# Attention and mLSTM stretch of a hybrid decoder layer: merge by quarters on two engines, masks and loads placed elsewhere

## Chip, cores and metric

One Trainium2 chip, one of its cores. The metric is the device time of one execution in microseconds (us). Engines: PE is TensorE (PEld its weight loads), DVE is VectorE, ACT is ScalarE, POOL is GpSimd, SP is SyncE, whose queue issues almost all DMAs of this kernel.

## What is computed

One layer for 2048 tokens of width 1024, all in float32. A combined projection of the normalised input feeds two groups: 8 attention heads of 128 with three dilated windows that are merged by their softmax denominators, and 4 mLSTM heads of 256 in chunks.

```python
u = jnp.einsum("bsd,de->bse", rmsnorm(x, norm_g), w_in)
q_a, k_a, v_a, z_a, x_m, o_m, z_m = jnp.split(u, cuts, axis=-1)
...
for window, dilation in ((128, 1), (512, 4), (2048, 16)):
    o, l = dilated_window_attention(heads(q_a), heads(k_a), heads(v_a), window, dilation, slopes)
wts = jax.nn.softmax(jnp.stack(lses), axis=0)
att = jnp.sum(wts[..., None] * jnp.stack(outs), axis=0).reshape(B, S, D_ATT)
att = att * jax.nn.silu(z_a)
...
hm = mlstm_chunkwise(mh(q_m), mh(k_m), mh(v_m), log_i, log_f)
hm = jax.nn.sigmoid(mh(o_m)) * hm
hm = (hm - mu) * lax.rsqrt(var + NORM_EPS) * hn_g
mls = hm.reshape(B, S, D_MLSTM) * jax.nn.silu(z_m)
return rmsnorm(x + jnp.einsum("bse,ed->bsd", jnp.concatenate([att, mls], -1), w_out), final_g)
```

## The kernel before

Three stages follow each other. The input projection (lines 348 to 520) leaves q, k, v, the gates and the mLSTM operands in DRAM. Then comes the stretch that the change is about: `attention` and `mlstm` are two Python generators, and the main loop takes one step of the first, then as many steps of the second as `total` (the number of steps that `mlstm` has) spreads over 204 of them. Last comes the output projection (lines 1078 to 1120).

**Attention.** A head has 32 steps: 16 blocks of queries, each once with its near keys and once with the strided ones, which hold the two longer windows in one row. A step makes the scores (`qk`, L741 to L747), turns the row two steps earlier over (`flip`, L755) and multiplies with v (`pv`, L773). The near part ends up in `oL`, the strided part in `oR`, both 128 x 2048. Three steps after a head is done `head_stats` turns the row sums over, sends them to DRAM and back in another order (`st_d`, `sL`, `sR`), and makes two weights for each token (`w`, L809), which go to DRAM (`wm_d`, L810). `head_merge` loads them back, copied to all 128 partitions (`wb`, L820), in two halves of 1024 tokens. For each half DVE does four operations of 128 x 1024: `oL` times its weight (L824), `oR` times its weight (L826), their sum (L829), and the gate `zs` times the sum (L834), which reads and writes every fourth element; then `att_d` is stored (L835). `wb` is one buffer, so the second half is loaded when the first has been used. The merge of a head runs while the next head's steps go on.

**mLSTM.** There are 16 chunks of 128 tokens, and two units in each, of two heads. `load` (L912 to L923) fetches five operands from DRAM: `v`, `q`, `xc`, `nb` (two rows of gate numbers copied to all partitions) and `ot`. `unit` makes a causal mask on GpSimd (`E`, L930), takes its exponential on ScalarE (L934), scales q on GpSimd (`qs`, L937), multiplies the mask with the scores (L944), and does the products with the state `C` (L961 to L981). `norm` finishes a chunk: small DVE operations on 128 x 4 (L987 to L999, with `rsqrt`, L84 to L93), four `hm` scalings of 128 x 256 (L1003), then per unit the load of the gate `z` (L1009), four transposes on PE (L1013), a product on DVE (L1014) and a store (L1015).

The order on each engine is set by a scheduler at build time, from the order in which the code issues the instructions and from its own durations. On the chip each engine and the SP queue go through their lists in that order: an instruction that waits holds up all that stand behind it on its engine. All tiles are guarded by semaphores that the build puts in.

The lines that the prediction speaks of most:

```python
820  nc.sync.dma_start(wb[:, i], wm_d[h][i:i + 1, :]...[:, :, cs].to_broadcast([128, 4, 256]))
826  nc.vector.tensor_tensor(v, v, wb[:, 1], ALU.mult)
834  nc.vector.tensor_tensor(zq, zq, o.rearrange("p r q -> p q r"), ALU.mult)
930  nc.gpsimd.affine_select(E, nb[:, :, 0, :], pattern=[[0, 2], [1, 128]], ...)
1003 nc.vector.tensor_scalar(hm, hm, sm[:, 0, h:h + 1], sm[:, 3, h:h + 1], op0=ALU.add, op1=ALU.mult)
```

Of the kernel before, what the change touches and what calls it, by code (L numbers as in the profile page):

```python
# [16 lines left out]
T = 2048  # L17
# [10 lines left out]
def kernel(  # L28
# [782 lines left out]

    def head_merge(at, d):
        h = d["h"]
        oL, oR, zs = d["oL"], d["oR"], d["zs"]
        for hf in range(2):
            cs = slice(hf * 256, (hf + 1) * 256)
            t0 = hf * 1024
            wb = at.tile([128, 2, 4, 256], F32, name="wb")
            for i in range(2):
                nc.sync.dma_start(wb[:, i], wm_d[h][i:i + 1, :].rearrange("p (r q) -> p r q", r=4)[:, :, cs]  # L820
                                  .to_broadcast([128, 4, 256]))
# [5 lines left out]
            yield  # L827
# [4 lines left out]
            z = zs[:, t0:t0 + 1024]  # L832
            zq = z.rearrange("p (q r) -> p q r", r=4)
            nc.vector.tensor_tensor(zq, zq, o.rearrange("p r q -> p q r"), ALU.mult)  # L834
            nc.sync.dma_start(att_d[h][:, t0:t0 + 1024], z)  # L835
            yield

    def attention(at):
# [9 lines left out]
        for i in range(len(units) + 3):  # L848
            if i < len(units):
                h, u = units[i]  # L850
                if i == 0:
                    by_r.append(at.tile([128, 2, 2, 512], F32R, name="oL", bufs=2))
                    D_[0] = head_tiles(at, first_load)
                    D_[0]["kh"] = at.tile([128, T], F32R, name="wb")
                    qk_split(D_[0], 0)
                S_[i] = qk(at, D_[h], u)
# [31 lines left out]
            if merges and (i % 32 == 10 or i % 32 > 14) and next(merges[0], "end") == "end":  # L888
                merges.pop(0)
# [11 lines left out]
    def mlstm(mp):  # L901
        C = mp.tile([128, KT, 257], F32, name="C")
        L = {}
        Z = {}
# [3 lines left out]
        def load(c, p):  # L908
            cs = slice(c * 128, (c + 1) * 128)
            es = slice(4 * p, 4 * p + 4)  # L910
            v = mp.tile([128, 2, 257], F32, name="v", bufs=2)
            nc.sync.dma_start(v[:, :, 0:256], vm_d[cs, p * 512:(p + 1) * 512].rearrange("t (i d) -> t i d", i=2))  # L912
            nc.gpsimd.memset(v[:, :, 256:257], 1.0)
# [4 lines left out]
            nb = mp.tile([128, 2, 2, 128], F32, name="nb", bufs=2)  # L918
            for i in range(2):
                nc.sync.dma_start(nb[:, i].rearrange("p a t -> p (a t)"),  # L920
                                  nb_d[(2 * p + i) * 16 + c].rearrange("a t -> (a t)")[None, :].to_broadcast([128, 256]))
            ot = mp.tile([128, 512], F32, name="ot", bufs=2)
            nc.sync.dma_start(ot, o_d[cs, p * 512:(p + 1) * 512])  # L923
            L[c, p] = (v, q, xc, nb, ot)

        def unit(c, p):
            v, q, xc, nb, ot = L.pop((c, p))
            sm = SM[c]
            E = mp.tile([128, 2, 128], F32, name="E")
            nc.gpsimd.affine_select(E, nb[:, :, 0, :], pattern=[[0, 2], [1, 128]], compare_op=ALU.is_ge,  # L930
                                    fill=-BIG, base=0, channel_multiplier=-1)
            for i in range(2):
                j = (2 * p + i) * 16 + c
                nc.scalar.activation(E[:, i], E[:, i], AF.Exp, bias=gcol[:, 0, j:j + 1])  # L934
            if c:
                qs = mp.tile([128, 4, 128], F32, name="qs")
                nc.gpsimd.tensor_tensor(qs.rearrange("p (i e) t -> p i e t", e=2), q.rearrange("p (i e) t -> p i e t", e=2),  # L937
                                        nb[:, :, 1, None, :].to_broadcast([128, 2, 2, 128]), ALU.mult)
# [6 lines left out]
            yield  # L945
            if c < NB - 1:
# [24 lines left out]
            for i in range(2):  # L971
                j = (2 * p + i) * 16 + c
                for e in range(2):
                    if c < NB - 1:
# [5 lines left out]
                        else:  # L980
                            nc.vector.tensor_copy(ce, u[:, 0:257])  # L981
                    yield

        def norm(c):
            sm = SM[c]
            hms = [HM.pop((c, p)) for p in range(2)]
            nc.vector.reciprocal(sm[:, 1, :], sm[:, 1, :])  # L987
# [17 lines left out]
            cs = slice(c * 128, (c + 1) * 128)  # L1005
            for p in range(2):
                es = slice(4 * p, 4 * p + 4)
                z = mp.tile([128, 4, 128], F32, name="z", bufs=2)
                nc.sync.dma_start(z, zm_d[es, :, cs].rearrange("e p t -> p e t"))  # L1009
                yield  # L1010
# [3 lines left out]
                nc.vector.tensor_tensor(z, z, ps, ALU.mult)  # L1014
                nc.sync.dma_start(mls_d[es, :, cs].rearrange("e p t -> p e t"), z)  # L1015
                yield

        load(0, 0)
        tail = None
        for c in range(NB):  # L1020
            SM[c] = mp.tile([128, 4, MH], F32, name="sm", bufs=2)
            for p in range(2):
                nxt = (c, 1) if p == 0 else (c + 1, 0)
                if nxt[0] < NB:
                    load(*nxt)
                for n, _ in enumerate(unit(c, p)):
# [11 lines left out]

# [43 lines left out]
    def out_fin(pss, b):  # L1082
        xr = at.tile([128, 2, D], F32, name=("zs", "wb")[b % 2])[:, 0]
# [22 lines left out]
    def out_last(pss, b):  # L1106
        xr = at.tile([128, 2, D], F32, name=("zs", "wb")[b % 2])[:, 0]
# [153 lines left out]
```

## Time and profile before

| | |
|---|---|
| time, median of 3 runs | 2215.12 us (2212.78 to 2215.84) |
| the profiled execution | 2221.72 us |
| span of its instructions | 2219.9 us |
| busy: PE, DVE, ACT, POOL | 2101.2 (95%), 1466.3 (66%), 923.1 (42%), 173.2 (8%) us |
| mean granted TensorE clock | 0.983 of full speed |
| DMA | 332.70 MB, mean 150 GB/s |

Busy time is an average over the stages. Attention and mLSTM run from about 1241 to 1800 us of the span; the last head and the first products of the output projection reach to about 1905 us. A row of the chain of waits names what ended each wait; idle time of PE is what the sections below look for.

### The profile page before, as it was taken

The page shows a single profiled execution, that of the slowest core. Times are in us where ns is not written, and L with a number is a line of the kernel's source. Part 1 is how long each engine was busy: PE and PEld are TensorE (multiplying, and loading weights), DVE is VectorE, ACT ScalarE, POOL GpSimd, SP SyncE. Part 2 cuts the span into 40 slices and gives each one's busy share as a digit, 9 for nine tenths or more (in the row PEclk, how much of TensorE's full clock was granted, in tenths as well). Part 3 has the DMA queues.
Part 4 walks back from the last instruction along what each step waited for, and adds up shares of the span by engine and source line. Part 5 has one row for each costly group of instructions (what it writes and reads, how often), then busy time and mean ns, then how long its engine had stood idle before and what let it go on. Part 6 is the DMA issues. An engine that isn't in the chain of part 4 may idle for free.

```text
span 2219.9 us, 32081 instructions
## 1 busy us (share of the span) xinstructions
PE 2101.2 (95%) x11762; PEld 1780.5 (80%) x11762; DVE 1466.3 (66%) x2969; ACT 923.1 (42%) x1873; POOL 173.2 (8%) x187
## 2 busy tenths in 40 slices
PE   5999999999999999999999898998889979899998
PEld 4677878998888888787789887888888877788886
DVE  8888767656696458586666567877877866442322
ACT  6433333333383223334344565665565664211111
POOL 2200000000000000000000212222222210000000
PEclk9999999999999999999999999999999999999999
DMA  4255343433253333343324767878779846543221
GB/s 153 95 177 188 114 158 119 154 115 109 81 204 133 114 114 107 123 143 121 122 77 159 192 169 224 239 217 238 196 220 238 224 152 196 158 133 95 95 91 38
DMA packets 300717, 332.70 MB, mean 150 GB/s; under 512 B 19536, under 2 KB 241168, under 8 KB 298512
## 3 DMA queue, kind: packets, MB, share of 16 engines
q1 hardware_dynamic: 299696, 330.06, 47.9%
q8 instruction: 93, 1.52, 0.3%
q10 hardware_dynamic: 864, 0.59, 0.1%
q14 instruction: 64, 0.52, 0.1%
HBM read 221.87 MB, written 108.72 MB: 149 GB/s over the span
## 4 chain that ended last, share of the span: by engine, by line
PE 76%; DVE 9%; DMA 8%; ACT 3%; issue 2%; SPq 1%; POOL 1%; ACTq 0%; DVEq 0%; POOLq 0%
PE pb L348 34%; PE pa L348 13%; PE pm L773 3%; DMA wb<-wm_d 2%; PE pt L755 2%; DMA nb<-nb_d 1%; PE pu L1078 1%; PE pu L1079 1%; PE pu L1080 1%; PE aux L493 1%; PE aux L503 1%; PE pt L1080 1%; PE pt L1078 1%; PE pt L1079 1%; PE pq L1080 1%
## 5 line engine op out<-in xcount | busy, mean ns | idle before, releaser
L97 ACT ACTIVATE whi<-ws 128x1024 fp32r<-128x1024 f32 x140 | 148.2, 1059 | 377.7 <-PE pb L348 211.8
L98 DVE TENSOR_TENSOR wlo<-ws,whi 128x1024 fp32r<-128x1024 f32 x140 | 171.9, 1228 | 81.7 <-ACT whi L97 81.6
L138 DVE TENSOR_TENSOR ws<-w,w 128x1024 f32<-128x1024 f32 x140 | 172.2, 1230 | 24.9 <-DMA w<-in_w_in 23.2
L747 ACT ACTIVATE s<-s,st 128x256 f32<-128x256 f32 (+3 forms) x256 | 134.9, 527 | 82.6 <-DVE st L745 75.3
L410 DVE TENSOR_TENSOR o<-pb,o 128x1024 f32<-128x1024 f32 x84 | 102.8, 1224 | 95.0 <-PE pb L348 93.9
L745 DVE CUSTOM_DVE_ANT_0 s<-pq,bl 128x256 f32<-128x256 f32 (+3 forms) x256 | 114.4, 448 | 39.1 <-PE pq L743 18.3
L755 PE MATMUL pt<-sc,s 128*128 128x128 f32 x568 | 109.7, 284 | 22.2 <-DVE E L944 7.3
L97 ACT ACTIVATE whi<-w 128x1024 fp32r<-128x1024 f32 x56 | 59.2, 1057 | 123.0 <-PE pb L348 116.6
L760 ACT ACTIVATE p<-pt 128x256 f32<-128x256 f32 (+1 forms) x192 | 80.9, 422 | 70.2 <-PE pt L755 68.0
L410 DVE TENSOR_TENSOR o<-pa,o 128x1024 f32<-128x1024 f32 x56 | 68.4, 1221 | 61.4 <-PE pa L348 61.4
L755 PEld LDWEIGHTS pt<-sc,s 128*128 128x128 f32 x568 | 72.8, 145 | 34.1 <-ACT p L760 9.1
L773 PE MATMUL pm<-p,vc 128*128 128x128 f32 x640 | 97.2, 283 | 2.1 <-ACT p L760 1.3
L605 POOL COPY bl<-bl 128x256 f32<-128x256 f32 x8 | 6.1, 757 | 1136.9 <-DMA q<-q_d 1111.6
L976 PE MATMUL pu<-v,kw 128*128 128x257 f32 x240 | 74.2, 404 | 19.9 <-DVE C L979 13.9
L403 ACT ACTIVATE o<-pb 128x1024 f32<-128x1024 f32 x84 | 85.0, 1017 | 17.2 <-DVE o L410 9.5
L773 PEld LDWEIGHTS pm<-p,vc 128*128 128x128 f32 x640 | 85.3, 198 | 5.2 <-ACT p L760 3.2
L98 DVE TENSOR_TENSOR wlo<-w,whi 128x1024 fp32r<-128x1024 f32 x56 | 68.3, 1220 | 27.5 <-ACT whi L97 27.5
L773 PE MATMUL pm<-p,vn 128*128 128x128 f32 x496 | 80.0, 283 | 2.8 <-ACT p L760 2.8
L482 DVE SCALAR_TENSOR_TENSOR y<-o,cw,y 128x512 f32<-128x512 f32 x96 | 72.1, 751 | 2.5
L773 PEld LDWEIGHTS pm<-p,vn 128*128 128x128 f32 x496 | 68.3, 197 | 4.9 <-ACT p L760 4.7
L348 PE MATMUL pa<-h4h,whi 128*128 128x512 f32 x160 | 66.8, 417 | 1.0 <-ACT h4h L97 1.0
L348 PE MATMUL pa<-h7l,whi 128*128 128x512 f32 x160 | 64.1, 401 | 2.4 <-DVE h7l L98 2.4
(730 smaller groups left out, 6501.4 us busy)
## 6 DMA issues: line engine op xcount, KB each, us to landing
w<-in_w_in SPq DMA_DIRECT2D x112, 512.0 KB
wb<-wm_d SPq DMA_DIRECT2D x32, 512.0 KB
q_d<-o SPq DMA_DIRECT2D x8, 1024.0 KB
k_d<-o SPq DMA_DIRECT2D x16, 512.0 KB
vm_d<-vm SPq DMA_DIRECT2D x32, 256.0 KB
xc_d<-xc SPq DMA_DIRECT2D x32, 256.0 KB
qm_d<-qm SPq DMA_DIRECT2D x32, 256.0 KB
v_d<-o SPq DMA_DIRECT2D x8, 1024.0 KB
```

Source lines behind the costliest of these rows:

```text
L97: nc.scalar.activation(hi, raw, AF.Copy)
L98: nc.vector.tensor_tensor(lo, raw, f(hi), ALU.subtract)
L138: eng.tensor_tensor(s, a, b, ALU.add if sign > 0 else ALU.subtract)
L348: nc.tensor.matmul(out, lhsT, rhs, start=start, stop=stop, skip_group_check=True)
L403: nc.scalar.activation(dst, order(ps), AF.Copy)
L410: nc.vector.tensor_tensor(dst, ps, src, op)
L745: nc.vector.tensor_tensor_reduce(s[:, :n], ps[:, :n], bias, 1.0, 3e38, ALU.add, ALU.min, accum_out=st[:, col:col + 1])
L747: nc.scalar.activation(s[:, :n], s[:, :n], AF.Exp, bias=st[:, col:col + 1], scale=-1.0, accum_out=st[:, 16 + col:17 + col])
L755: nc.tensor.transpose(pp[:, i * 128:(i + 1) * 128], s[:, i * 128:(i + 1) * 128], ident)
L760: nc.scalar.activation(p[:, :n], pp[:, :n], AF.Copy)
L773: nc.tensor.matmul(od, v, p[:, j * 128:(j + 1) * 128], start=j == 0, stop=j == m - 1)
L976: nc.tensor.matmul(u[:, 0:257], kw[:, 2 * i + e, :], v[:, i], start=True, stop=True)
```

## The change

The merge of a head goes by four quarters of 512 tokens (`weights_load`, L812 to L816, and `head_merge`). `wb` has two smaller buffers; the first two quarters are loaded before any is used, the others when a buffer is free. `oL` times its weight and the sum stay on DVE (now L831 and L839, 128 x 512); `oR` times its weight and the gate times the sum go to GpSimd (L832 and L842). The store of a quarter is issued in the next one (L837, L844). The merge goes on at every step from the tenth of a head.

In `mlstm`, `load` is issued after the second step of the unit before, in the order `nb`, `q`, `xc`, `v`, `ot` (L925 to L934); `v` has two fixed buffers, whose column of ones is set once and not each time. The mask and `qs` move from the unit's start into `prepare` (L940, L944), called late in the unit before, with two buffers each. `norm` loads `z` at its start (L1010), scales `hm` on GpSimd (L1028), and issues its stores (L1038) two steps later. `total` follows: a chunk now has 26 steps and not 25. The keys' copy `kh` of the first head, and two tiles of the last stage, take other buffers.

```diff
+    def weights_load(at, d, n):
+        wb = d["wb", n] = at.tile([128, 2, 4, 128], F32, name="wb", bufs=2)
+        for i in range(2):
+            nc.sync.dma_start(wb[:, i], wm_d[d["h"]][i:i + 1, :].rearrange("p (r q) -> p r q", r=4)
+                              [:, :, n * 128:(n + 1) * 128].to_broadcast([128, 4, 128]))
...
-        for hf in range(2):
...
-            wb = at.tile([128, 2, 4, 256], F32, name="wb")
...
-            nc.vector.tensor_tensor(o, o, wb[:, 0], ALU.mult)
-            yield
-            nc.vector.tensor_tensor(v, v, wb[:, 1], ALU.mult)
...
-            nc.vector.tensor_tensor(o, o, v, ALU.add)
...
-            nc.vector.tensor_tensor(zq, zq, o.rearrange("p r q -> p q r"), ALU.mult)
-            nc.sync.dma_start(att_d[h][:, t0:t0 + 1024], z)
+        weights_load(at, d, 0)
+        yield
+        weights_load(at, d, 1)
+        yield
+        yield
+        for n in range(4):
...
+            nc.vector.tensor_tensor(o, o, wb[:, 0], ALU.mult)
+            nc.gpsimd.tensor_tensor(v, v, wb[:, 1], ALU.mult)
+            yield
+            if n < 2:
+                weights_load(at, d, n + 2)
+            if n:
+                nc.sync.dma_start(att_d[h][:, (n - 1) * 512:n * 512], zs[:, (n - 1) * 512:n * 512])
+            yield
+            nc.vector.tensor_tensor(o, o, v, ALU.add)
+            zq = zs[:, ts].rearrange("p (q r) -> p r q", r=4)
+            yield
+            nc.gpsimd.tensor_tensor(zq, zq, o, ALU.mult)
+            yield
+        nc.sync.dma_start(att_d[h][:, 1536:2048], zs[:, 1536:2048])
...
-            if merges and (i % 32 == 10 or i % 32 > 14) and next(merges[0], "end") == "end":
+            if merges and i % 32 >= 10 and next(merges[0], "end") == "end":
...
+        V = [mp.tile([128, 2, 257], F32, name=f"v{n}") for n in range(2)]
+        for v in V:
+            nc.gpsimd.memset(v[:, :, 256:257], 1.0)
...
+        def prepare(c, p):
+            q, nb = L[c, p][1], L[c, p][3]
+            E = mp.tile([128, 2, 128], F32, name="E", bufs=2)
+            nc.gpsimd.affine_select(E, nb[:, :, 0, :], ...)
+            qs = mp.tile([128, 4, 128], F32, name="qs", bufs=2)
+            if c:
+                nc.gpsimd.tensor_tensor(qs..., q..., nb[:, :, 1, None, :]..., ALU.mult)
...
             nc.vector.tensor_tensor(E, E, ps[:, 0:2, :], ALU.mult)
             yield
+            if nxt:
+                load(*nxt)
...
+                    if nxt and i == 1 and e == 0:
+                        prepare(*nxt)
                     yield
...
+            for p in range(2):
+                z = mp.tile([128, 4, 128], F32, name="z", bufs=2)
+                nc.sync.dma_start(z, zm_d[4 * p:4 * p + 4, :, cs].rearrange("e p t -> p e t"))
...
-                nc.vector.tensor_scalar(hm, hm, sm[:, 0, h:h + 1], sm[:, 3, h:h + 1], op0=ALU.add, op1=ALU.mult)
+                nc.gpsimd.tensor_scalar(hm, hm, sm[:, 0, h:h + 1], sm[:, 3, h:h + 1], op0=ALU.add, op1=ALU.mult)
...
-    total, done, start, end, lag = 16 * 25, 0, 18, 222, 5
+    total, done, start, end, lag = 16 * 26, 0, 18, 222, 5
```

What the build makes of it is seen in the engines' lists. DVE, the merge of the fourth head (its first half before, its first quarter now), before:

```order
L824 TENSOR_TENSOR oL<-oL,wb 128x4x256
L745 ISA s,st<-pq,bl 128x256
L745 ISA st 128x1
L826 TENSOR_TENSOR oR<-oR,wb 128x4x256
L965 SCALAR_TENSOR_TENSOR hm,sm<-ot,pu 128x256
L968 SCALAR_TENSOR_TENSOR sm<-pu,gcol 128x1
L997 TENSOR_SCALAR sm<-sm 128x4
```

and now:

```order
L831 TENSOR_TENSOR oL<-oL,wb 128x4x128
L745 ISA s,st<-pq,bl 128x256
L745 ISA st 128x1
L1021 SCALAR_TENSOR_TENSOR sm<-sm 128x4
L839 TENSOR_TENSOR oL<-oL,oR 128x4x128
L959 TENSOR_TENSOR E<-E,pt 128x256
```

L826 and L834 are gone from this list; the sum L839 stands one step (one L745) behind the product, and it takes `oR` from GpSimd.

GpSimd, the first merge and the unit before it, now (before, only the mask, `qs`, the casts L616 and a memset stood here):

```order
L1028 TENSOR_SCALAR hm<-hm,sm 128x256 x4
L940 AFFINE_SELECT E<-nb 128x256
L944 TENSOR_TENSOR qs<-q,nb 128x512
L832 TENSOR_TENSOR oR<-oR,wb 128x4x128 x2
L842 TENSOR_TENSOR zs<-zs,oL 128x4x128
L616 COPY qr<-qh 128x512
L832 TENSOR_TENSOR oR<-oR,wb 128x4x128
L842 TENSOR_TENSOR zs<-zs,oL 128x4x128
L616 COPY qr<-q 128x512
L832 TENSOR_TENSOR oR<-oR,wb 128x4x128
L842 TENSOR_TENSOR zs<-zs,oL 128x4x128
L940 AFFINE_SELECT E<-nb 128x256
```

The casts of q for the strided rows and the next mask now stand between and behind operations that wait for `wb` and for DVE.

SP, from the store of the fourth head's weights on, before:

```order
L810 DMA wm_d_85<-w 64x2x32
L1015 DMA mls_d<-z 128x4x128
L1009 DMA z<-zm_d 128x4x128
L915 DMA q<-qm_d 128x4x128
L820 DMA wb<-wm_d_85 128x4x256 x2
L1015 DMA mls_d<-z 128x4x128
L912 DMA v<-vm_d 128x2x256
L917 DMA xc<-xc_d 128x4x128
L920 DMA nb<-nb_d 128x256 x2
```

and now:

```order
L810 DMA wm_d_85<-w 64x2x32
L1038 DMA mls_d<-z 128x4x128
L925 DMA nb<-nb_d 128x256 x2
L815 DMA wb<-wm_d_85 128x4x128 x4
L1038 DMA mls_d<-z 128x4x128
L815 DMA wb<-wm_d_85 128x4x128 x2
L1010 DMA z<-zm_d 128x4x128 x2
L928 DMA q<-qm_d 128x4x128
L930 DMA xc<-xc_d 128x4x128
L932 DMA v_10237<-vm_d 128x2x256
L934 DMA ot<-o_d 128x512
```

`nb` goes first and `v` late; the third quarter of `wb`, which waits for a free buffer, stands ahead of the loads of the next unit.

## Rows read from the trace of the kernel before

**Rows 1.** Windows by stage; clock and DMA are means of each stretch.
```profile
core 0: us, PE busy (x) PEld busy (x) DVE busy (x) ACT busy (x) POOL busy (x), PEclk, DMA share, GB/s
0.00:1241.00 1241.00, 1209.06 (x6634) 1008.51 (x6634) 861.65 (x1034) 483.54 (x621) 25.92 (x22) 1.00 0.38 130
1241.00:1800.00 559.00, 495.69 (x3330) 449.57 (x3330) 426.49 (x1509) 334.23 (x1009) 143.11 (x162) 0.96 0.80 219
1800.00:1905.00 105.00, 90.05 (x478) 73.79 (x477) 66.74 (x135) 52.67 (x124) 4.15 (x4) 0.93 0.60 190
1905.00:2219.90 314.90, 306.38 (x1325) 248.59 (x1323) 111.45 (x294) 52.68 (x119) 0.00 (x0) 0.99 0.29 95
```
**Rows 2.** Who waited for whom, PE, 1241 to 1800: total us, times, longest.
```profile
PE pu L976 <- DVE C L979: 13.9, 8, 5.2
PE pt L755 <- DVE E L944: 7.3, 3, 4.6
PE pt L755 <- ACT p L760: 7.0, 5, 3.4
...
PE pt L1013 <- DVE hm L1003: 2.3, 1, 2.3
```
**Rows 3.** Groups of instructions by shape, DVE, 1241 to 1800: busy us, mean ns.
```profile
L1003 DVE TENSOR_SCALAR hm<-hm,sm 128x256 f32<-128x256 f32 x64 | 26.0, 461 | 0.3
L834 DVE TENSOR_TENSOR zs<-zs,oL 128x1024 f32<-128x1024 f32 x12 | 25.3, 2111 | 0.0
...
L826 DVE TENSOR_TENSOR oR<-oR,wb 128x1024 f32<-128x1024 f32 x12 | 16.4, 1364 | 0.3 <-DMA wb<-wm_d 0.3
L824 DVE TENSOR_TENSOR oL<-oL,wb 128x1024 f32<-128x1024 f32 x12 | 16.0, 1336 | 10.7 <-DMA wb<-wm_d 10.7
...
L92 DVE SCALAR_TENSOR_TENSOR rs_y<-rs_t,rs_y 128x4 f32<-128x4 f32 x48 | 10.3, 216 | 0.8
```
**Rows 4.** Groups of instructions by shape, POOL, 1241 to 1800.
```profile
L937 POOL TENSOR_TENSOR qs<-q,nb 128x512 f32<-128x512 f32 x30 | 41.7, 1390 | 2.6 <-POOL E L930 2.5
L616 POOL CAST qr<-qh 128x512 fp32r<-128x512 f32 x28 | 36.5, 1302 | 139.1 <-PE pq L742 94.2 <-PE pq L743 28.1 <-ACT qh L613 5.9
...
L930 POOL TENSOR_SCALAR_AFFINE_SELECT E<-nb 128x256 f32<-128x256 f32 x32 | 19.9, 623 | 133.3 <-DMA nb<-nb_d 23.1 <-PE pu L961 21.5 <-DMA q<-q_d 18.0
```
**Rows 5.** Who waited for whom, all engines, 1241 to 1800.
```profile
ACT E L934 <- POOL E L930: 45.4, 24, 5.8
...
DVE z L1014 <- DMA z<-zm_d: 7.1, 5, 2.5
```
**Rows 6.** The chain of waits, two pieces of the first merge: start, us, what.
```profile
1331.44 6.34 DMA wm_d<-w
1337.81 4.37 DMA wb<-wm_d
```
**Rows 7.** Timeline, PE, from 1343: start, us, what, [idle before <-releaser].
```profile
1343.87 0.80 PE L976 MATMUL pu<-v,kw 128*128 128x257 f32 x1 [5.20 <-DVE C L979]
```
**Rows 8.** Timeline, DVE and POOL, 1294 to 1298.
```profile
1294.58 0.16 DVE L92 SCALAR_TENSOR_TENSOR rs_y<-rs_t,rs_y 128x4 f32<-128x4 f32 x1
...
1295.66 1.08 DVE L92 SCALAR_TENSOR_TENSOR rs_y<-rs_t,rs_y 128x4 f32<-128x4 f32 x1
...
1295.39 1.33 POOL L616 CAST qr<-qh 128x512 fp32r<-128x512 f32 x1 [3.99 <-PE pq L742]
```
**Rows 9.** Timeline, SP, POOL and ACT, 1655 to 1663: one mask.
```profile
1655.66 1.07 SPq L920 DMA_DIRECT2D nb<-nb_d  x2
...
1662.42 0.41 POOL L930 TENSOR_SCALAR_AFFINE_SELECT E<-nb 128x256 f32<-128x256 f32 x1 [11.90 <-DMA ot<-o_d]
...
1662.86 0.69 ACT L934 ACTIVATE E<-E,gcol 128x128 f32<-128x128 f32 x2 [4.22 <-POOL E L930]
```
**Rows 10.** Who waited for whom, SP's own queue, 1241 to 1800.
```profile
SPq L1015 <- DVE z L1014: 53.7, 15, 9.5
SPq L912 <- PE pu L976: 38.3, 13, 9.0
```

More of the change, by code (lines that the diff above doesn't have):

```diff
@@ L910, in load @@
             es = slice(4 * p, 4 * p + 4)
-            v = mp.tile([128, 2, 257], F32, name="v", bufs=2)
-            nc.sync.dma_start(v[:, :, 0:256], vm_d[cs, p * 512:(p + 1) * 512].rearrange("t (i d) -> t i d", i=2))
-            nc.gpsimd.memset(v[:, :, 256:257], 1.0)
+            nb = mp.tile([128, 2, 2, 128], F32, name="nb", bufs=2)
+            for i in range(2):
+                nc.sync.dma_start(nb[:, i].rearrange("p a t -> p (a t)"),
+                                  nb_d[(2 * p + i) * 16 + c].rearrange("a t -> (a t)")[None, :].to_broadcast([128, 256]))
             q = mp.tile([128, 4, 128], F32, name="q", bufs=2)
@@ L917, in load, with unit @@
             nc.sync.dma_start(xc, xc_d[es, :, cs].rearrange("e p t -> p e t"))
[L918 to L921, printed above, removed]
+            v = V[p]
+            nc.sync.dma_start(v[:, :, 0:256], vm_d[cs, p * 512:(p + 1) * 512].rearrange("t (i d) -> t i d", i=2))
             ot = mp.tile([128, 512], F32, name="ot", bufs=2)
             nc.sync.dma_start(ot, o_d[cs, p * 512:(p + 1) * 512])
[L924 to L929, printed above, removed]
+            L[c, p] = [v, q, xc, nb, ot]
+        def prepare(c, p):
+            q, nb = L[c, p][1], L[c, p][3]
+            E = mp.tile([128, 2, 128], F32, name="E", bufs=2)
             nc.gpsimd.affine_select(E, nb[:, :, 0, :], pattern=[[0, 2], [1, 128]], compare_op=ALU.is_ge,
                                     fill=-BIG, base=0, channel_multiplier=-1)
+            qs = mp.tile([128, 4, 128], F32, name="qs", bufs=2)
+            if c:
+                nc.gpsimd.tensor_tensor(qs.rearrange("p (i e) t -> p i e t", e=2), q.rearrange("p (i e) t -> p i e t", e=2),
+                                        nb[:, :, 1, None, :].to_broadcast([128, 2, 2, 128]), ALU.mult)
+            L[c, p] += [E, qs]
+        def unit(c, p, nxt):
+            v, q, xc, nb, ot, E, qs = L.pop((c, p))
+            sm = SM[c]
             for i in range(2):
@@ L1023, in mlstm @@
                 nxt = (c, 1) if p == 0 else (c + 1, 0)
-                if nxt[0] < NB:
-                    load(*nxt)
-                for n, _ in enumerate(unit(c, p)):
+                for n, _ in enumerate(unit(c, p, nxt if nxt[0] < NB else None)):
                     yield
@@ L1082, in out_fin @@
     def out_fin(pss, b):
-        xr = at.tile([128, 2, D], F32, name=("zs", "wb")[b % 2])[:, 0]
+        xr = at.tile([128, D], F32, name="zs") if b % 2 == 0 else at.tile([128, D], F32, name="wb", bufs=2)
         nc.sync.dma_start(xr, x[b * 128:(b + 1) * 128, :])
@@ L1106, in out_last @@
     def out_last(pss, b):
-        xr = at.tile([128, 2, D], F32, name=("zs", "wb")[b % 2])[:, 0]
+        xr = at.tile([128, D], F32, name="zs") if b % 2 == 0 else at.tile([128, D], F32, name="wb", bufs=2)
         nc.sync.dma_start(xr, x[b * 128:(b + 1) * 128, :])
```

34 lines of the change are left out of this document (11 added, 23 removed).

## Prediction

> **What bounds the kernel now.** I read the windows by stage first [rows 1]. PE is busy for 97% of the first 1241 us and of the last 315 us, and nothing that the change moves lies there. Between 1241 and 1800 us PE is busy for 495.7 of 559.0 us: 63.3 us idle. Its mean granted clock there is 0.96 (of the two levels, 2.4 GHz and 1.2 GHz, it fell to the lower now and then, each time after a longer stall), and (1 - 0.96) x 559 = 22 us of PE's work went that way. So about 85 us are to be had in this stretch, and 15 us of idleness more in the 105 us behind it. No engine is full there (DVE 76%, ACT 60%, POOL 26%), but the DMA engines are busy for 80% of it, so that loads land late and in bursts.
>
> Next, who PE waited for [rows 2]. Twelve rows of the answer name DVE, from the 13.9 us shown down to 0.3, 42.2 us together; four name ACT, from 7.0 to 2.8, together 18.2; GpSimd 1.8. Behind DVE stand two things. The first is a transfer on which DVE itself stood: 10.7 us for the merge weights `wb` [rows 3], 7.1 for `z` [rows 5]. The longest idle time of PE, 5.20 us [rows 7], is one of these: the weights' store took 6.34 us and their load 4.37 us [rows 6], and the state update that PE needed stood behind L824 in DVE's list. The other, 42.2 - 17.8 = 24 us, is DVE's own queue. Behind ACT stands the mask: ACT waited 45.4 us in 24 places for `E` [rows 5]. One case in full [rows 9]: `nb` is issued from 1655.66 on, the mask runs at 1662.42, and ACT, which then stood 4.22 us, had other exponentials behind it.
>
> **The change part by part**, against the profiled execution (2221.72 us, 6.6 us above the median of 2215.12; savings are taken off the median).
>
> *Work moved off DVE.* It loses L834 (12 x 2.11 = 25.3), L826 (16.4) and L1003 (64 x 0.46 = 26.0) [rows 3]: 67.7 us of 426.5. The merge's other two operations come as quarters; the same elements in twice the instructions, some 2 us more. GpSimd gets 24 products L832 at 1.39, as L937 [rows 4]: 33 us. It gets 24 products L842, strided in and out: no such row exists, so the bounds are 1.39 (two plain inputs) and 1.39 + 1.30 (the strided cast L616 on top) [rows 4]; I take 2.0, the middle: 48 us. And 64 scalings at 0.62, as the mask of the same size [rows 4]: 40 us. The memsets saved are 3. That makes 143 + 118 = 261 us, 47% of the stretch. The page GPSIMD Engine Reference of the Trainium skill (sections Performance versus the Vector engine and Performance pitfalls for Q7 kernels) has 4497 ns for a two-input operation of 2048 elements and half as much again for reads with a step above 8 bytes, an estimate of 1.7 us for L842, and advises VectorE for such work; by it GpSimd would be at 254 us and the sum below the same.
>
> *The two engines hold each other up.* While a cast ran on GpSimd from 1295.39, a DVE operation of 128 x 4 that takes 0.16 us took 1.08 [rows 8]; over 48 of its kind the mean is 0.216 [rows 3], so 0.056 more each with GpSimd busy 26% of the time. At 47% that becomes 0.10; for 19 small operations x 16 chunks it is 304 x 0.045 = 14 us of DVE's time (none if they miss each other, 40 if each meeting costs half a cast of 1.30, 304 x 0.21 x 0.65). DVE keeps 67.7 - 2 - 14 = 52 us: from 76% busy to 67%. The free share goes from 24 to 33%, and I take 40% of the 24 us of queueing as gone: **10 us** (between 3, the share of DVE's own time, 12% of 24, and all 24).
>
> *`z` loaded at the norm's start.* In SP's order the load now stands five attention steps or more ahead of its use in all but the last pair; before, it was one step in 18 of 32 cases. DVE's 7.1 us go; PE feels under half of such waits: **3 us** (0 to 7).
>
> *Masks and loads.* `nb` now goes first in its group, and SP should stand less: it waited 53.7 us for the `z` that it was to store and 38.3 us for `v`'s buffer [rows 10], with the next loads behind. But the loads are issued a step or more later, and the build puts the mask right behind: one step after `nb` at most in 28 of 32 units, against 15 before; a step is 559/216 = 2.6 us, and the case of [rows 9] took 5 to 7 us. A mask that is "ahead" in the code is still awaited on ACT. Between all of ACT's 18 us gone and half as much added I take **4 us**, nearer to nothing.
>
> *`wb` in quarters.* Between L809 and the first product DVE now has three or four steps for most heads, where it had four or five; the chain to the weights needs 6.3 + 4.4 us [rows 6]. The pieces are half as large and the second wait for one buffer goes. I take **0** (5 lost to 6 won). SP's wait for the third quarter holds up the loads behind it, which have four steps or more before use; that covers it, and if not, each of seven heads loses the 1.4 us of the product that frees the buffer, 10 us. Of GpSimd, which PE now meets through `hm` and DVE through L839, I charge **-3 us** (0 to -10): `hm` has 4 to 5 steps before its transposes in most chunks.
>
> *Clock.* 22 us were lost with 63 us of idleness, so 14 us less idle time gives back **5 us**. The last stage and the stretch from 1800 to 1905 stay: the last merge, DVE's 13 us, is now about 12 us on GpSimd in a row with DVE.
>
> Sum: 10 + 3 + 4 + 0 - 3 + 5 = 19 us, so 2215 - 19 = **2196 us**; with the bounds, 2182 to 2209.
>
> **The rivals.**
> *GpSimd becomes the gate (slower).* Masks, q casts and `hm` stand in one list with products that wait for `wb` and for DVE. If `nb` or `wb` lands later than GpSimd reaches it, the wait is passed to ACT (mask), to DVE (L839) and to PE (`hm`). For it: one step from `nb` to the mask, and 5 to 7 us of landing [rows 9]. Against it: `nb` goes first. It decides where `nb` lands over 4 us after its issue in most units: then 32 x 3 us of waiting on ACT instead of 45, at 18.2/45.4 of PE time per us, add 20 us, GpSimd's own waits 10 and the clock 3; less the 13 us of the first two terms: 2235 us.
> *The relief is eaten (no change).* The Trainium skill, page SBUF — State Buffer (section Who interferes with whom), says that the second of two such instructions stands until the first has ended. As a mechanism of this kernel: at the upper bound of 40 us DVE keeps 26 of the 67.7 us, its term is 5, and with the masks at 0 and GpSimd at -6 the rest cancels: 2213 us. For it: 1.08 against 0.16 [rows 8]; against it: the mean of 48 is only 0.216 [rows 3].
> *Most stalls go (much faster).* If `nb` first and an unblocked SP bring the loads in time, ACT's 18.2 and DVE's 24 mostly vanish: 33 us of idleness and 12 of clock: 2170 us.
>
> **How the numbers follow.** A measurement of this kernel tells 0.2% (4.4 us) from no change. The forecast has 0.56, the fast rival 0.12, no change 0.12, the gate 0.20. So faster 0.68, within 0.2% 0.12, slower 0.20. The range is 2164 to 2226: it holds the forecast, no change and nearly all of the fast rival, and leaves out the gate's greater part, some 0.15. The faster cases alone span 2164 to 2209.
>
> **What would show it.** Right: DVE busy near 375 us in this stretch and GpSimd near 260; PE waits for DVE near 28 us in total, none of them behind `z`; a clock mean of 0.97. The masks: ACT's wait for `E` still above 30 us. Wrong: PE waiting for `hm` on GpSimd or DVE for GpSimd's `oR` with more than 10 us would be the gate; small DVE operations with a mean above 0.3 us would be the eaten relief; ACT's wait for `E` under 15 us would be the fast rival. L842 far over 2.7 us would put the whole GpSimd sum wrong.

## The result and the profile after

The changed kernel takes 2238.16 us (median of 4 runs, 2233.37 to 2241.66) against 2215.48 us before (4 runs): a ratio of 1.0101, 95% interval 1.0078 to 1.0125. It is slower by 22 us; 19 us faster were forecast, and the range ended at 2226. The profiled execution is 2241.66 us with a span of 2239.9 us, 20.0 us more than before.

First where in the span. The last scores of the last head on DVE, in the timeline of the kernel before and then of the changed one (start, us, what, idle time before it and its releaser):

```profile
1848.60 0.69 DVE L745 CUSTOM_DVE_ANT_0 s<-pq,bl 128x512 f32<-128x512 f32 x1 [1.38 <-PE pq L743]
```

```profile
1860.47 0.69 DVE L745 CUSTOM_DVE_ANT_0 s<-pq,bl 128x512 f32<-128x512 f32 x1 [0.83 <-PE pq L743]
```

Up to there the change has lost 11.9 us; the other 8.1 us are lost behind the last head, where nothing was charged. Now the stretch from 1241 to 1800 us, in the windows of the changed kernel (columns as in [rows 1]):

```profile
1241.00:1800.00 559.00, 491.84 (x3299) 450.05 (x3297) 398.69 (x1428) 327.32 (x994) 238.96 (x243) 0.94 0.82 219
```

PE is busy for 491.84 us at a mean granted clock of 0.94; before it was 495.69 at 0.96, and did more of its work in that time (3330 matmul records against 3299). So PE stands 4 us more, while the lower clock alone, 0.02 of 559 us, is, as an estimate, 11 us of PE's work. DVE is busy for 28 us less and GpSimd for 96 more. Who PE waited for there (compare [rows 2]):

```profile
PE pt L966 <- DVE E L959: 16.0, 9, 5.3
PE pt L1034 <- DVE E L959: 8.4, 3, 5.7
PE pu L993 <- DVE C L996: 8.3, 3, 3.7
PE pu L993 <- DVE sm L986: 6.7, 5, 3.4
PE pq L741 <- DVE st L745: 5.9, 3, 5.0
PE pt L755 <- DVE sm L1014: 5.1, 2, 4.6
PE pt L755 <- ACT p L760: 4.9, 5, 2.5
...
PE pt L1034 <- POOL hm L1028: 3.0, 1, 3.0
```

The rows that name DVE are 54 us now (42.2 before), those that name ACT 6.2 (18.2 before). PE's waits for ACT became shorter, as the fast rival wanted; those for DVE became longer, though DVE does less. ACT's own wait for the masks fell too, from the 45.4 us of [rows 5]:

```profile
ACT E L953 <- POOL E L940: 30.9, 14, 5.3
```

PE's two largest rows name `E`, the mask times the scores (L959), with 24.4 us. One of these waits in full, from the timelines of PE, DVE and POOL (columns as in [rows 7]):

```profile
1506.98 1.09 PE L1034 MATMUL pt<-sc,hm 128*128 128x128 f32 x4 [5.66 <-DVE E L959]
```

```profile
1501.16 0.69 DVE L831 TENSOR_TENSOR oL<-oL,wb 128x512 f32<-128x512 f32 x1 [2.96 <-DMA wb<-wm_d]
...
1504.14 0.69 DVE L839 TENSOR_TENSOR oL<-oL,oR 128x512 f32<-128x512 f32 x1 [1.56 <-POOL oR L832]
1504.75 1.75 DVE L831 TENSOR_TENSOR oL<-oL,wb 128x512 f32<-128x512 f32 x1
1506.43 0.41 DVE L959 TENSOR_TENSOR E<-E,pt 128x256 f32<-128x256 f32 x1
```

```profile
1502.84 1.26 POOL L832 TENSOR_TENSOR oR<-oR,wb 128x512 f32<-128x512 f32 x1 [2.98 <-DMA wb<-wm_d]
1504.58 1.37 POOL L832 TENSOR_TENSOR oR<-oR,wb 128x512 f32<-128x512 f32 x1 [0.47 <-DMA wb<-wm_d]
```

DVE stood 2.96 us for `wb`, then 1.56 us for GpSimd, which itself had stood 2.98 us for its half of `wb`; and the next product took 1.75 us where 0.69 is usual, for GpSimd's second product ran from 1504.58 to 1505.95. That is 2.96 + 1.56 + 1.06 = 5.6 us, PE's 5.66. Before, PE's longest stand, 5.20 us [rows 7], held one wait, for `wb`. By the Trainium skill, page SBUF — State Buffer (section Who interferes with whom), the second of two such instructions stands until the first has ended; the 1.75 us agree (1505.95 and 0.69 more would be 1506.64, and the product ended at 1506.50).

Behind the last head the quarters go from engine to engine with nothing beside them. DVE, POOL and PE of the changed kernel:

```profile
1888.72 0.69 DVE L839 TENSOR_TENSOR oL<-oL,oR 128x512 f32<-128x512 f32 x1 [1.93 <-POOL oR L832]
...
1892.70 0.69 DVE L839 TENSOR_TENSOR oL<-oL,oR 128x512 f32<-128x512 f32 x1 [2.69 <-POOL oR L832]
```

```profile
1891.38 1.29 POOL L832 TENSOR_TENSOR oR<-oR,wb 128x512 f32<-128x512 f32 x1
1893.47 1.93 POOL L842 TENSOR_TENSOR zs<-zs,oL 128x512 f32<-128x512 f32 x1 [0.80 <-DVE oL L839]
```

```profile
1918.49 1.22 PE L1098 MATMUL pu<-vn,k 128*128 128x512 f32 x2 [13.96 <-ACT k L97]
```

A quarter takes 4.0 to 4.4 us there, and PE then stands 13.96 us for the attention rows of the output projection; in the kernel before the same wait is 7.24 us, 6.7 less:

```profile
1897.80 1.22 PE L1078 MATMUL pu<-vn,k 128*128 128x512 f32 x2 [7.24 <-ACT k L97]
```

What the operations cost, in the groups by shape of POOL and DVE from 1241 to 1800 us (compare [rows 3, 4]):

```profile
L842 POOL TENSOR_TENSOR zs<-zs,oL 128x512 f32<-128x512 f32 x24 | 40.0, 1670 | 9.0 <-DVE oL L839 3.9 <-DVE rs_t L91 2.9 <-DVE sm L1022 2.1
L1028 POOL TENSOR_SCALAR hm<-hm,sm 128x256 f32<-128x256 f32 x64 | 37.8, 604 | 62.7 <-DVE sm L1024 58.6 <-ACT kw L970 4.2
L832 POOL TENSOR_TENSOR oR<-oR,wb 128x512 f32<-128x512 f32 x24 | 33.5, 1395 | 26.0 <-DMA wb<-wm_d 26.0
```

```profile
L831 DVE TENSOR_TENSOR oL<-oL,wb 128x512 f32<-128x512 f32 x24 | 22.7, 944 | 17.2 <-DMA wb<-wm_d 17.2
L839 DVE TENSOR_TENSOR oL<-oL,oR 128x512 f32<-128x512 f32 x24 | 20.5, 856 | 9.6 <-POOL oR L832 9.5
L92 DVE SCALAR_TENSOR_TENSOR rs_y<-rs_t,rs_y 128x4 f32<-128x4 f32 x48 | 14.5, 302 | 1.1
```

### The profile page after: what moved, and what is told of

Read it like the earlier page. It is cut to its first block, busy times and chain, and to the rows that moved or that the text cites. A ratio compares the mean times of both kernels' runs of the same rounds, so it can differ in the third digit from the quotient of the medians.

```text
span 2239.9 us, 32211 instructions
## 1 busy us (share of the span) xinstructions
PE 2105.5 (94%) x11762; PEld 1786.3 (80%) x11762; DVE 1436.5 (64%) x2905; ACT 920.4 (41%) x1873; POOL 296.3 (13%) x285
## 4 chain that ended last, share of the span: by engine, by line
PE 71%; DMA 11%; DVE 9%; issue 3%; POOL 3%; ACT 2%; SPq 1%; ACTq 0%; DVEq 0%; POOLq 0%
PE pb L348 31%; PE pa L348 12%; PE pm L773 2%; DMA wb<-wm_d 2%; DMA nb<-nb_d 1%; PE pu L1098 1%; PE aux L493 1%; PE aux L503 1%; PE pu L1100 1%; PE pu L1099 1%; PE pt L755 1%; PE pt L1100 1%; PE pt L1098 1%; PE pt L1099 1%; PE pq L1100 1%
## 5 line engine op out<-in xcount | busy, mean ns | idle before, releaser
L745 DVE CUSTOM_DVE_ANT_0 s<-pq,bl 128x256 f32<-128x256 f32 (+3 forms) x256 | 114.1, 448 | 38.7 <-PE pq L743 16.4
L98 DVE TENSOR_TENSOR wlo<-w,whi 128x1024 fp32r<-128x1024 f32 x56 | 68.3, 1220 | 27.5 <-ACT whi L97 27.5
L348 PE MATMUL pa<-h4l,whi 128*128 128x512 f32 x160 | 64.5, 403 | 2.6 <-DVE h4l L98 2.6
```

What stands on the lines that cost most here:

```text
L98: nc.vector.tensor_tensor(lo, raw, f(hi), ALU.subtract)
L348: nc.tensor.matmul(out, lhsT, rhs, start=start, stop=stop, skip_group_check=True)
L745: nc.vector.tensor_tensor_reduce(s[:, :n], ps[:, :n], bias, 1.0, 3e38, ALU.add, ALU.min, accum_out=st[:, col:col + 1])
```

## The experiments

Three theories stood against each other for the 22 us. **Gate**: GpSimd's list holds products that wait, with masks and `hm` behind them, and DVE waits for GpSimd. **Late loads**: the mLSTM loads, issued later, bring the masks late. **Blocking**: GpSimd's time as such slows DVE. Ratios are to the kernel before in runs on the same chip; 0.1% is 2.2 us.

**The two parts alone.** First the changed kernel with the whole function `mlstm` as it was, so that only the merge is changed:

```diff
-    total, done, start, end, lag = 16 * 26, 0, 18, 222, 5
+    total, done, start, end, lag = 16 * 25, 0, 18, 222, 5
```

> The kernel before with the merge of the change alone (quarters, two products on GpSimd); the mLSTM part as before. Three theories for the 22 us. Gate: masks and hm stand behind waiting merge products in GpSimd's list; here hm is on DVE and the masks are made at the unit's start, so about half of the loss is left: 2222 to 2230 us, with ACT waiting over 45 us for E. Late loads: the loss is from the mLSTM loads, issued later; here they are as before, so only the longer last merge (about 8 us) is seen: 2220 to 2225 us, and PE waits for DVE's E product stay under 10 us. Blocking: GpSimd's work slows DVE; GpSimd has some 70 us more here, so 2220 to 2228 and small DVE operations of 128x4 with a mean over 0.25 us.

Measured 1.0149 (1.0122 to 1.0176). Then the kernel before with the whole `mlstm` of the change and its 26 steps:

```diff
-    total, done, start, end, lag = 16 * 25, 0, 18, 222, 5
+    total, done, start, end, lag = 16 * 26, 0, 18, 222, 5
```

> The kernel before with the mLSTM part of the change alone (masks ahead, loads and stores later, hm on GpSimd, 26 steps); the merge as before, in halves on DVE. Gate: GpSimd's list has no product that waits for the merge weights, so the masks come in time and z early helps: 2200 to 2213 us, ACT's wait for E under 25 us. Late loads: the masks still wait for nb, which is issued only a few steps ahead: 2222 to 2232 us, GpSimd's wait for nb about 60 us as in the changed kernel, PE waiting over 15 us for DVE's E product. Blocking: 40 us of hm on GpSimd: 2210 to 2218 us.

Measured 0.9930 (0.9908 to 0.9952), 2206.03 us. So the merge costs some 33 us alone and the mLSTM part gains 15. The mLSTM part as a whole, later loads included, is not where the loss is; what its later loads cost by themselves is tried below. The run with the mLSTM part alone fell into the gate theory's range (2200 to 2213), but not by its mechanism: ACT waited 40.3 us for `E`, where under 25 was named. For the merge alone the gate theory named 7 to 15 us and blocking 5 to 13, both too little. The way through the masks is not seen: ACT waited 48.5 us for `E` in that run, hardly more than the 45.4 of [rows 5]. The sign of blocking is there: the 304 operations of 128 x 4 on DVE took 91.2 us, and 64.7 in the kernel before; what GpSimd's time as such costs is tried below with spare work.

**All three moved operations back on DVE, and the two merge products alone:**

```diff
-            nc.gpsimd.tensor_tensor(v, v, wb[:, 1], ALU.mult)
+            nc.vector.tensor_tensor(v, v, wb[:, 1], ALU.mult)
...
-            nc.gpsimd.tensor_tensor(zq, zq, o, ALU.mult)
+            nc.vector.tensor_tensor(zq, zq, o, ALU.mult)
...
-                nc.gpsimd.tensor_scalar(hm, hm, ...)
+                nc.vector.tensor_scalar(hm, hm, ...)
```

> The changed kernel with all three moved operations (both merge products and the hm scaling) on DVE; quarters, masks ahead and later loads stay. Gate and blocking both: the loss goes, 2208 to 2218 us. Late loads: 2228 to 2240 us, with PE's wait for DVE's E product still over 15 us and GpSimd's wait for nb over 60 us. If DVE's relief was worth anything, this is slower than the run with hm alone on GpSimd.

Measured 0.9994 (0.9978 to 1.0010).

> The changed kernel with the two merge products back on DVE, hm scaling still on GpSimd. Gate: the masks no longer stand behind products that wait for the merge weights: 2205 to 2218 us; PE's wait for DVE's E product under 8 us (24 in the changed kernel). Late loads: 2228 to 2240 us. Blocking: half way, 2222 to 2230 us. In all of them the last merge has no hand-over between engines any more, which gives back some of the 8 us behind the last head.

Measured 1.0009 (0.9995 to 1.0022). The two products on GpSimd cost 0.9%, 20 us. With them back on DVE, PE's two rows for `E` (24.4 us in the changed kernel) come to 16.8 us, not to the 8 that were named, and in the stretch from 1241 to 1800 us PE is busy for 498.14 us and the clock is back at 0.96:

```profile
1241.00:1800.00 559.00, 498.14 (x3371) 453.42 (x3372) 418.29 (x1511) 337.78 (x1027) 175.36 (x197) 0.96 0.83 219
```

The scaling of `hm` on GpSimd wins nothing: with 26 us more on DVE the kernel is no slower. And quarters on DVE (1.0009) are still 0.8% behind halves on DVE (0.9930).

**Why the quarters on DVE lose.** First an attempt to start them later:

```diff
-            if merges and i % 32 >= 10 and next(merges[0], "end") == "end":
+            if merges and (i % 32 in (0, 10, 11) or i % 32 > 13) and next(merges[0], "end") == "end":
```

> The changed kernel with its merge held two steps: the first two quarters are still loaded at the steps 10 and 11 of a head, the first products come at step 15 as in the kernel before (13 now). If the merge loses because its products reach DVE and GpSimd before the weights have landed (35 us of GpSimd's waits and 18 of DVE's), both fall under a third and the ratio to before goes from 1.010 to 1.000 to 1.004. If the hand-over between the two engines or GpSimd's work as such costs the time, it stays at 1.008 or above. The tail behind the last head is untouched: some 370 us from the last scores to the end, as in the changed kernel (362 before).

Measured 1.0090 (1.0061 to 1.0119), but it tests little: the build drew the products forward again. In DVE's list the first product stands 3, 3, 4, 4, 4, 4, 5 steps (one L745 each) behind the weights, against 3, 3, 4, 3, 3, 4, 5 in the changed kernel. So the other way round, halves that start early, in the kernel with the mLSTM part alone:

```diff
-            if merges and (i % 32 == 10 or i % 32 > 14) and next(merges[0], "end") == "end":
+            if merges and i % 32 >= 10 and next(merges[0], "end") == "end":
```

> The kernel with the mLSTM part alone, its halves taken at every step from the tenth of a head on, as the change takes the quarters: the first product stands one step earlier in DVE's list (2 to 4 steps behind the weights and not 3 to 6). If the early start is why the quarters on DVE (1.001) lose to the halves on DVE (0.993), the ratio rises to 0.997 to 1.002 and DVE's wait for the weights grows from 15 to over 25 us. If the quarters themselves do it, it stays at 0.992 to 0.995.

Measured 1.0011 (0.9999 to 1.0023), with 2, 3, 3, 3, 4, 3, 5 steps against 3, 4, 4, 4, 5, 4, 6. That is the whole 0.8%: the early start costs 18 us, and the quarters as such nothing that these runs can tell (1.0009 against 1.0011, with the halves a step earlier than the quarters in three of seven heads and a step later in one). The edit moves the first product and all that follows in the merge, so the 18 us are not the price of the first product's step alone. DVE's wait for the weights, 1241 to 1800 us, in the halves as they were and then started early (total us, times, longest):

```profile
DVE oL L824 <- DMA wb<-wm_d: 14.1, 5, 4.7
```

```profile
DVE oL L824 <- DMA wb<-wm_d: 23.1, 6, 5.5
```

These 9 us more, a little less than the expectation named (25 us in all), are half of the 18. ACT's wait for `E` grew as well, from 40.3 to 49.7 us, and PE's for `hm` from 3.7 to 9.6.

**What a product on GpSimd costs.** In halves, with the mLSTM part alone:

```diff
-            nc.vector.tensor_tensor(v, v, wb[:, 1], ALU.mult)
+            nc.gpsimd.tensor_tensor(v, v, wb[:, 1], ALU.mult)
```

> The kernel with the mLSTM part alone (ratio 0.993), merge in halves, with the product of oR by its weight on GpSimd (14 operations of 128x1024, some 2.7 us each, 38 us). If a product on GpSimd that waits for the weights is what harms, by holding up masks and q casts, the ratio rises to 0.998 to 1.003. If only the ping-pong of quarters between the engines harms, this stays at 0.991 to 0.995 or wins 2 us from the shorter DVE list.

Measured 1.0036 (1.0016 to 1.0055), a little above the range named: 1.1% for one product, without quarters. The masks are not its way: ACT's wait for `E` is 27.5 us there, and 40.3 with the product on DVE. PE's two largest rows name `E` on DVE again (8.5 and 2.4 us in the kernel without the move):

```profile
PE pt L956 <- DVE E L949: 11.6, 7, 3.9
PE pt L1024 <- DVE E L949: 7.8, 4, 3.9
```

Then spare work on GpSimd in place of the product:

```diff
             nc.vector.tensor_tensor(v, v, wb[:, 1], ALU.mult)
+            for _ in range(8):
+                nc.gpsimd.tensor_tensor(dm[0], ident, ident, ALU.mult)
```

> The kernel with the mLSTM part alone (ratio 0.993), all merge products on DVE, and beside each product of oR eight products of 128x128 on GpSimd that nobody waits for and that wait for nothing (some 40 us of GpSimd's time in all). If GpSimd's time as such is what a moved product costs (it holds up DVE's operations and the masks in its own list), the ratio rises as with the real product, to 1.000 to 1.004. If the waits do it (GpSimd for the weights, DVE for GpSimd), this stays at 0.992 to 0.996.

Measured 1.0156, and spoilt: the build put all 128 operations in one row ahead of the first masks (53.4 us), and PE stood 48.0 us there once. The who-waits row of PE:

```profile
PE pt L959 <- DVE E L952: 56.0, 8, 48.0
```

and the block on GpSimd, in its groups:

```profile
L828 POOL TENSOR_TENSOR dm<-sc 128x128 bf16<-128x128 f32 x128 | 53.4, 417 | 9.6
```

It shows only that a mask behind GpSimd's work stops PE. Tied to the merge by its data:

```diff
             nc.vector.tensor_tensor(v, v, wb[:, 1], ALU.mult)
+            for r in range(6):
+                nc.gpsimd.tensor_tensor(dm[0], v[:, r // 2, r % 2 * 128:r % 2 * 128 + 128], ident, ALU.mult)
```

> As the run with spare work on GpSimd, but tied: behind each product of oR on DVE, GpSimd makes six products of 128x128 that read its result into a spare tile; nobody waits for them (some 40 us in all, in 16 places). If GpSimd's time as such costs, 0.998 to 1.004; if it is the waits between the engines, 0.992 to 0.996.

Measured 0.9968 (0.9955 to 0.9981), between both. GpSimd's spare work, in its groups from 1241 to 1800 us:

```profile
L828 POOL TENSOR_TENSOR dm<-oR,sc 128x128 bf16<-128x128 f32 x72 | 49.6, 689 | 25.6 <-DVE oR L826 21.3
```

So 50 us of GpSimd's time in this stretch (78 in the whole kernel, not the 40 that were meant) that nobody waits for cost 0.4% (8 us), while 31 us (41 in the whole kernel) of a product that DVE waits for cost 1.1% (23 us). The waits are the larger part. Last, the two products of the changed kernel taken apart: only the gate on GpSimd, and only the product of `oR`.

```diff
-            nc.gpsimd.tensor_tensor(v, v, wb[:, 1], ALU.mult)
+            nc.vector.tensor_tensor(v, v, wb[:, 1], ALU.mult)
```

> The changed kernel with the product of oR back on DVE; the gate times the sum stays on GpSimd (48 us of its work), so that no operation on DVE waits for GpSimd any more. If the hand-over to DVE (product, then sum) is the loss, the ratio falls from 1.010 to 1.000 to 1.003, that of both products on DVE. If GpSimd's time is the loss, it stays at 1.005 or above.

Measured 1.0026 (1.0008 to 1.0043): 0.2% above both on DVE. Nobody but a store waits for the gate.

```diff
-            nc.gpsimd.tensor_tensor(zq, zq, o, ALU.mult)
+            nc.vector.tensor_tensor(zq, zq, o, ALU.mult)
```

> The changed kernel with the gate (z times the sum) back on DVE; only the product of oR is on GpSimd. With the run that has only the gate on GpSimd at 1.0026 and both on DVE at 1.0009: if the hand-over from GpSimd to DVE is the loss, this is at 1.006 to 1.011, DVE's wait for oR 8 us or more; if it takes both products to crowd GpSimd's list, 1.002 to 1.005.

Measured 1.0040 (1.0025 to 1.0054): 0.3% above both on DVE, in the second of the two ranges, and DVE's wait is 5.2 us, under the 8 named:

```profile
POOL oR L832 <- DMA wb<-wm_d: 46.3, 22, 4.7
...
DVE oL L839 <- POOL oR L832: 5.2, 4, 2.0
```

Together the two cost 0.9%, more than 0.2 + 0.3 (by a little more than the intervals allow). With both, the next product of `oR` stands behind the gate, which waits for DVE's sum, and DVE's next sum waits for that product: a loop over two engines, as the last merge shows it (4.0 to 4.4 us a quarter). That the loop is what makes up the difference was not tried by itself.

**What the mLSTM part gains.** Its pieces, each alone:

```diff
-                nc.gpsimd.tensor_scalar(hm, hm, ...)
+                nc.vector.tensor_scalar(hm, hm, ...)
```

> The kernel with the mLSTM part alone, hm scaling back on DVE. If the relief of DVE by 26 us is where the gain of this part comes from, the ratio rises from 0.993 to 0.997 to 1.000. If the gain is from the order (z early, stores late, masks ahead), it stays at 0.991 to 0.995 (with hm on GpSimd costing as much in hand-over as it saves).

Measured 0.9920 (0.9894 to 0.9946): DVE's relief is no part of the gain.

```diff
+            if nxt:
+                load(*nxt)
             for i in range(2):
                 nc.scalar.activation(E[:, i], E[:, i], AF.Exp, ...)
...
-            if nxt:
-                load(*nxt)
             if c < NB - 1:
```

> The kernel with the mLSTM part alone, its five loads issued at the unit's start and not after the second step. If the mask is still late because nb is issued too late (GpSimd waits 84 us for nb there, ACT 40 us for E), these waits halve and the ratio falls from 0.993 to 0.987 to 0.991. If SP's list, not the place of the load, decides when nb lands (the loads then stand behind other transfers or wait for buffers), it stays within 0.991 to 0.996.

Measured 0.9881 (0.9853 to 0.9909). ACT's wait halves, GpSimd's for `nb` does not (83.6 us, then 70.5). The mask's wait on ACT, with the loads late and then early:

```profile
ACT E L943 <- POOL E L930: 40.3, 16, 6.1
```

```profile
ACT E L945 <- POOL E L930: 21.1, 12, 3.7
```

So issuing the loads two steps later costs some 11 us. The fixed buffers of `v` alone, in the kernel before:

```diff
-            v = mp.tile([128, 2, 257], F32, name="v", bufs=2)
-            nc.gpsimd.memset(v[:, :, 256:257], 1.0)
+            v = V[p]
```

> The kernel before with fixed buffers for v alone: no memset in GpSimd's list (it waited 85 us there for the matmuls that free the buffer, with the next mask behind it). If that wait is what made the masks late, ACT's wait for E falls from 45 to under 30 us and the ratio is 0.993 to 0.997. If the masks then only wait for nb, 0.998 to 1.001.

Measured 1.0003 (0.9990 to 1.0016): nothing. The norm of the change alone, `hm` on DVE, and then its two edits apart:

```diff
+            for p in range(2):
+                nc.sync.dma_start(z, zm_d[4 * p:4 * p + 4, :, cs]...)
             nc.vector.reciprocal(sm[:, 1, :], sm[:, 1, :])
...
-                nc.sync.dma_start(z, zm_d[es, :, cs]...)
...
-                nc.sync.dma_start(mls_d[es, :, cs]..., z)
                 yield
+                yield
+                nc.sync.dma_start(mls_d[4 * p:4 * p + 4, :, cs]..., zs[p])
```

> The kernel before with the norm of the change alone, hm scaling on DVE: z loaded at the norm's start, stores two steps later, 26 steps. SP waited 54 us there for the z that it was to store, with loads behind it, and DVE 7 us for z. If this frees SP and so the masks, 0.992 to 0.996; if only DVE's 7 us are won, 0.998 to 1.000.

Measured 0.9900 (0.9875 to 0.9925): all of the gain, and more; it is below the range that was named for SP (0.992 to 0.996).

> The run with the norm of the change alone (0.990), but with each store issued right behind its product, as before: z early remains. If SP's stand for the z to be stored is what held the loads up, that stand comes back (53.7 us before, 12.1 with the later stores) and the ratio is 0.996 to 1.000. If the early z is the gain, 0.989 to 0.993.

Measured 0.9900 (0.9879 to 0.9920).

> The kernel before with each store issued two steps behind its product and z loaded where it was. If SP's stand for the z to be stored held the loads up, it falls under 20 us and the ratio is 0.990 to 0.995. If the early z is the gain, DVE's wait for z stays near 7 us and the ratio is 0.997 to 1.001.

Measured 0.9955 (0.9939 to 0.9970), between the two ranges, and neither sign came: SP's stand is 32.2 us and not under 20, DVE's wait for `z` 3.3 and not 7:

```profile
SPq L1017 <- DVE z L1014: 32.2, 10, 8.4
DVE z L1014 <- DMA z<-zm_d: 3.3, 2, 3.0
```

So the later stores alone gave some 10 us, the early `z` alone 22, and both no more than 22. The run with the later stores is not quite clean: its edit makes 27 steps of a chunk, while `total` counts 26, so the last 16 steps are issued in one go. The early `z` comes with a 26th step, and what a step more does by itself was not tried; against the later stores the early `z` is worth 12 us, so 12 to 22 is what these runs give it. SP's stand for the product that is to be stored was not what mattered beside the early `z`; there it was back (32.2 us too, and more rows of its kind) and the time was not. In the kernel with the early `z` DVE's wait for `z` [rows 5] is gone, and ACT waits less for the masks than the 45.4 us of [rows 5]:

```profile
ACT E L934 <- POOL E L930: 30.2, 20, 3.5
```

**A version that beats both.** The mLSTM part of the change with its loads at the unit's start and `hm` on DVE, the merge of the kernel before:

> The version that should beat both: mLSTM part of the change, its loads at the unit's start, hm scaling on DVE, merge in halves on DVE. From the two single steps (0.988 and 0.992 against 0.993) a ratio of 0.986 to 0.990.

Measured 0.9864 (0.9843 to 0.9885), 2189.16 us: as expected, though its interval overlaps those of the runs with the earlier loads (0.9881) and with the norm alone (0.9900). Its stretch:

```profile
1241.00:1800.00 559.00, 508.83 (x3509) 463.49 (x3509) 443.40 (x1568) 352.89 (x1068) 141.15 (x135) 0.98 0.83 228
```

PE gets through more of its work here (3509 matmul records against 3330 before). DVE is busy for 443 us, more than before (426) and in the changed kernel (399), for more of its work, too, falls into this stretch; over the whole kernel it has 1459.8 us of work, against 1466.3 before and 1436.5 after the change. How busy DVE is was not the bound.

The staircase from before to after, one run for each step:

| step added | ratio | step, us |
|---|---|---|
| kernel before | 1.0000 | |
| `z` early (26 steps) | 0.9900 | -22 |
| stores later | 0.9900 | 0 |
| masks ahead, loads later, fixed `v` | 0.9920 | +4 |
| `hm` on GpSimd | 0.9930 | +2 |
| merge starts early (halves) | 1.0011 | +18 |
| quarters, on DVE | 1.0009 | 0 |
| gate on GpSimd | 1.0026 | +4 |
| product of `oR` on GpSimd: the change | 1.0101 | +17 |

Each ratio has an interval of 0.1 to 0.25% to either side, so steps of 4 us and less are not told from none. The steps depend on their order. The product of `oR` on GpSimd costs 17 us on top of the gate, 7 on quarters without it, and 23 on halves that start late: the early start and the product share a part of their loss, and no line of the staircase is a price by itself.

## Why the prediction was wrong, step by step

- **Work moved off DVE (10 us forecast)** failed, and with it the reading of [rows 2] as a queue that shrinks with DVE's load. `hm` back on DVE changed nothing, and the fastest version has as much work on DVE as the kernel before. GpSimd's durations were near: 1.395, 1.670 and 0.604 us against 1.39, 2.0 and 0.62, in sum 239 us against 261 forecast. The prediction's estimate of 1.7 us for L842, worked out from the Trainium skill's page GPSIMD Engine Reference (sections Performance versus the Vector engine and Performance pitfalls for Q7 kernels), agrees with the 1.670. DVE fell to 398.7 us and not to 375. Quarters of L831 and L839 took 43.2 us against 31.4 for the halves, where 2 us more were charged: 48 quarters of the usual 0.69 us would be 33.1, and with both merge products back on DVE they took 34.7, so 8.5 us came with GpSimd's products, as in the 1.75 us above.
- **Engines that hold each other up (14 us of DVE)** was near: the 304 small operations take 85.2 us now and took 64.7, 20.5 more (L92 at 302 ns against 216). With the quarters' 12 us and smaller shifts, DVE's busy time fell by 28 of the 67.7 us moved, near the 26 of the rival whose relief is eaten, and L92 is at that rival's sign of 0.3 us. Its time, 2213 us, was still wrong: what DVE keeps is not what sets the time.
- **`z` early (3 us)** was mis-sized the other way: 12 to 22 us. The sum took DVE's 7.1 us as the upper bound. But DVE stands in order, and ACT's waits for the masks fell too when `z` came early. How the one reaches the other was not followed to the end.
- **Masks and loads (4 us)**: 4 us lost, within the bounds. It hides two opposite things: the later loads cost about 11 us, so the masks ahead, with early loads, may be worth something (0.9864 against 0.9900 without them, but the intervals overlap). ACT's wait for `E` stayed at 30.9 us, above the 30 forecast.
- **`wb` in quarters (0)** failed: 18 us lost, by the merge's earlier start. The prediction saw the cause, three or four steps where there were four or five, and put 5 us on it, to be met by smaller pieces. The smaller pieces gave nothing that the runs can tell.
- **GpSimd's waits (-3, bound -10)** failed: -20 us (1.0009 to 1.0101). The price was taken from `hm`, which turned out harmless (PE stood 3.0 us for it), not from DVE's wait in the sum, behind which stands `E`, which PE needs.
- **Last stage (0)** failed: 8.1 us lost. From the last scores to the end the span has 371.3 us before, 373.8 with both products on DVE and 379.4 after the change, so 5.6 of them belong to the 20. The prediction itself wrote that the last merge was now in a row with DVE, and charged nothing for it.
- **Clock (+5)**: the mean fell to 0.94, where 0.97 was forecast. PE was idle for 67.2 us of the 559 (63.3 before), where 14 us less was forecast. By the estimate above the lower clock is the larger part of what was lost in this stretch; with both merge products on DVE it is at 0.96 again.
- **The range.** The bounds of the terms, added up, go from 55 us won to 21 lost, 2160 to 2236 us before the clock. The stated 2182 to 2209 is much narrower, without a word on why, and the range, to 2226, left out an end that the terms allowed.

The rival that was right by its number, GpSimd as the gate at 2235 us, was right in one half of its mechanism only: DVE and GpSimd waiting for `wb` and for each other. The masks were not its way (ACT's wait fell from 45.4 to 30.9 us), and its signs stayed below their mark of 10 us (PE for `hm` 3.0, DVE for `oR` 9.5). That its number came out is luck: 20 of its 33 us were to come from the masks, where nothing was lost.

## What to carry to other kernels

An engine that stands in order is not relieved by less work if the work that is taken away comes back as a wait in its list: a chain whose steps go to and fro between two such engines cost 20 us, where each of its two moved products alone, the gate and the product of `oR`, cost 4 and 7. Ask of each load in the chain how far behind its producer its user stands; a merge that starts one step of 2.6 us earlier in every head cost 18 us, and `z` loaded some steps sooner gave 12 to 22. Where a scheduler draws work forward, look at the order that it made before an experiment is read.

## What was not expected of the hardware

The same products of 128x128 on GpSimd took 417 ns each in the block that was tied to nothing and 689 ns in the tied run, where DVE worked beside them (one input is another tile there). Of the 72 the median is 458 ns and the longest 2297, so it is a few that stand long. So GpSimd is slowed as well, not DVE alone. And a hand-over between DVE and GpSimd is not free of itself: in the last merge each GpSimd operation that waited for DVE's sum started 0.80 us after GpSimd's last one, the 0.69 us of the sum and 0.1 us more, so a quarter costs the sum of three operations, the product and the gate on GpSimd and the sum on DVE between them (1.29, 1.93 and 0.69 us); only the product of `oL` runs beside them.
